# A hybrid mLSTM and pooling block: the o and z projections of two heads as one group of 1024 columns, in which three of eight tile pairs are multiplied by seven products

## The chip, the core and the metric

The kernel runs on one core of one Trainium2 chip. The metric is the device time of one execution in microseconds (us). PE is the matmul engine (PEld its weight loads), DVE the vector engine, ACT the scalar engine, POOL the third elementwise engine, SP the engine whose queue issues the weight transfers. A matmul multiplies a stationary tile of 128x128 with up to 512 moving columns and adds the product to a bank of PSUM (128 x 512 float32).

## The reference, cut to what matters

256 tokens, width 2048, 8 heads of 256, float32 throughout.

```python
h = rmsnorm(x, norm_pre_w)
q, k, v, o_g, z_a, i_pre, f_pre, u_b, z_b, g_a, g_b = split(h @ w_in)   # 2048 columns each for q,k,v,o,z,g_a,g_b; 1024 for u,z_b
q, k = silu(causal_conv4(q)), silu(causal_conv4(k))
h_t  = mlstm_chunkwise(q * 256**-0.5, k, v, i_pre + bi, log_sigmoid(f_pre + bf))
h_t  = rmsnorm_per_head(h_t) * mlstm_norm_w
y_a  = sigmoid(o_g) * h_t * silu(z_a)
y_b  = (multiscale_pool(u_b) @ pool_w) * pool_scale * silu(z_b)
merged = sigmoid(g_a) * (y_a @ w_proj_mlstm) + sigmoid(g_b) * (y_b @ w_proj_pool)
x = x + rmsnorm(merged @ w_out, norm_post_w)
```

Here the chunkwise recurrence is computed with the 256 tokens as two halves of 128 (causal products of q, k and v with a decay matrix E).

## The kernel before

**Precision.** Every float32 operand is split into a high part `wh` (or `xh`) in the matmul's own float format and the remainder `wl` (`xl`), and a product is three matmuls: high with high, low with high, high with low. `hi_lo` does the splitting: ACT casts to the high part (L63), DVE subtracts (L64). The input x lies split in `xc` for the whole kernel (16 tiles of 128 channels, by 256 tokens).

**Weights.** They come as tiles `raw` of 128 x 2048 (1 MB), three of which rotate (`rawp`); SP's queue issues the transfers. Each tile is split in two chunks of 1024 columns; four `wh` and four `wl` rotate (`split`).

**Three ways to multiply.** `tok_block` makes 512 output columns for two halves of the tokens (`t` = 0, 1): x is stationary, the weights move, 96 matmuls (L127, L128, L130) into two `acc` banks. `chan_block` makes 256 output channels by 256 tokens: the weights are stationary, x moves, 64 wide and 64 half-wide matmuls (L147, L149). `group` makes 1024 columns for both halves of the tokens: eight tiles, each a pair of two 128-row blocks (from the upper and the lower half of the contraction) by two blocks of 512 columns. Five of the eight are multiplied plainly (24 matmuls each); three (`NS`) are multiplied by Winograd's form of Strassen's scheme, seven products instead of eight (21 matmuls): DVE forms differences of the four weight blocks (`t13`, `t24`, L673 to L675), the sums of the x blocks (`s_h`, `s_l`) are prepared once by `s_forms`, and the products go to four banks `ps` and four banks `C` and are combined at the end. The order of the eight is 3, 4, 0, 5, 1, 6, 2, 7: the form pairs 0, 1 and 2 stand between plain ones.

**The stages.** (1) `first`: o of heads 0 and 1, with x as it lands; meanwhile `stats` sums the squares of x on ACT (L249), POOL takes the power (`rstd`), and `stats_bc` spreads `rstd` over the partitions by two matmuls with a diagonal matrix `dg` (L264, L265). (2) Eight `chan_block`s for the pooling branch, beside them the gates' projection (`gates`, 16 matmuls of L291) and the pooling itself. (3) Four mLSTM stages j of two heads each, L573: o as a token block (in stage 0 it is there already), the first q block and its convolution (`conv_block`), z, the second q block, v, two k blocks; the attention-like part of the pair (`mlstm_pair`) is a generator that runs in steps between the chunks of the next stage and is emptied by `drain`. (4) Gates g_a and g_b, two token blocks and three groups; then the two projections, with two groups; then the output projection with the last group.

**What sets the order.** The kernel is written as a plain program; a scheduler then orders each engine's instructions by its own estimate of when their inputs are ready, and each engine takes its queue in that order. `tc.keep_in_program_order(i)` pins an instruction behind everything that was written before it on its engine. `const`, `rawp`, `ph1` and `latew` are pools of on-chip memory; a tile of a pool with `bufs=2` has two places that rotate.

Of the kernel before, what the change touches and what calls it, by code (L numbers as in the profile page):

```python
# [10 lines left out]
F32 = mybir.dt.float32  # L11
# [29 lines left out]
def block_kernel(ctx: ExitStack, tc: tile.TileContext, a: dict, out: bass.AP):  # L41
# [217 lines left out]
    def stats_bc():  # L259

        pb = small()
        for t in range(2):
            dg = sp.tile([P, P], F32, name="dg", bufs=2)
            nc.vector.tensor_scalar(dg, ident, rstd[:, t : t + 1], None, op0=ALU.mult)  # L264
            i = nc.tensor.matmul(pb[:, t * P : (t + 1) * P], ones_f, dg, start=True, stop=True)  # L265
            if t == 0:
                tc.keep_in_program_order(i)
        nc.vector.tensor_copy(rstd_bc, pb[:, :T])
# [217 lines left out]
    def mlstm_pair(j, G, qk):  # L486
# [38 lines left out]
        for hh in range(2):  # L525
# [46 lines left out]

    for j in range(4):  # L573
        po = tok_block(xtiles(4 + j), xh, xl) if j else so0
        so = []
        for t in range(2):
            s = gate.tile([P, 512], F32, name="g", tag=f"g{t}") if j else so0[t]
            nc.scalar.activation(s, po[t], AF.Sigmoid, scale=rstd[:, t : t + 1])
            so.append(s)
        pq = chan_block(qtiles(2 * j))  # L580
        drain()
        q = ph1.tile([P, 4, 2, T], F32R, name="q")
        qh, ql = q[:, :, 0], q[:, :, 1]
        kh, kl = (ph1.tile([P, 4, T], F32R, name=n) for n in ("kh", "kl"))
        conv_block(pq, 4 * j, qh, ql, 0)
        pz = tok_block(xtiles(8 + j), xh, xl)
        for t in range(2):
            s = ph1.tile([P, 512], F32, name="sz", tag="sz", bufs=2)
            nc.scalar.activation(s, pz[t], AF.Sigmoid, scale=rstd[:, t : t + 1])
            nc.vector.scalar_tensor_tensor(s, pz[t], rstd[:, t : t + 1], s, op0=ALU.mult, op1=ALU.mult)  # L590
            nc.vector.tensor_tensor(so[t], so[t], s, op=ALU.mult)
        conv_block(chan_block(qtiles(2 * j + 1)), 4 * j + 2, qh, ql, 2)
        pv = tok_block(xtiles(j), xh, xl)
        for t in range(2):
            hi_lo(
                v_h[:, t, :, 0:HD], v_l[:, t, :, 0:HD], pv[t].rearrange("p (h d) -> p h d", h=2),
                rstd[:, t : t + 1],
            )
        conv_block(chan_block(qtiles(8 + 2 * j)), 16 + 4 * j, kh, kl, 0)
        conv_block(chan_block(qtiles(8 + 2 * j + 1)), 16 + 4 * j + 2, kh, kl, 2)  # L600
        side.append(mlstm_pair(j, so, (q, kh, kl)))


    def st(tile_):
        return lambda k, t: tile_[:, k, t * P : (t + 1) * P]

# [17 lines left out]
    def group(gi, st_h, st_l, forms, get_a, get_b):  # L624
# [22 lines left out]
        for kp in order:  # L647
# [26 lines left out]
            nc.vector.tensor_tensor(t24[:, 0], b4[:, 3], t13[:, 0], op=ALU.subtract)  # L674
            nc.vector.tensor_tensor(t24[:, 1], b4[:, 2], t24[:, 0], op=ALU.subtract)  # L675
            flat = [t_.rearrange("p b n -> p (b n)") for t_ in (t13, t24)]
# [40 lines left out]
    for j in range(2):  # L717
        pg = tok_block(xtiles(12 + j), xh, xl)
        for t in range(2):
            gs[0, j, t] = gate.tile([P, 512], F32, name="g", tag=f"g{t}")  # L720
            nc.scalar.activation(gs[0, j, t], pg[t], AF.Sigmoid, scale=rstd[:, t : t + 1])  # L721
    drain()
    ph1_ctx.close()
    latew = ctx.enter_context(tc.tile_pool(name="latew", bufs=1, side="right"))
    lateg_ctx = ExitStack()
    lateg = lateg_ctx.enter_context(tc.tile_pool(name="lateg", bufs=1, side="right"))
    forms = s_forms(lambda part, h: xc[:, 8 * h : 8 * h + NS, part])
    for gi, (n, j0) in enumerate(((1, 0), (0, 2), (1, 2))):
# [10 lines left out]
    for jp in range(2):  # L739
# [184 lines left out]
```

## Time and profile before

| | |
|---|---|
| median of 3 runs | 970.8 us (970.52 to 970.91) |
| the profiled execution | 971.45 us, its span 969.6 us |
| mean granted clock of PE | 0.996 |
| weights read | 184.85 MB, 193 GB/s over the span |

The profiled execution is 0.65 us slower than the median. A line of a timeline has the start in us, the length in us, the engine, the line of the kernel, the operation, the tiles written and read with their shape, how many instructions were merged, and in brackets the idle time before it with what ended that. A row of a group has busy us and the mean ns of one; neighbours on one engine overlap a little, so the pitch from start to start is what counts in a sum.

### The profile page before, as it was taken

What the parts mean: (1) busy time and instruction counts of PE and PEld (TensorE: products, weight loads), DVE (VectorE), ACT (ScalarE), POOL (GpSimd) and SP (SyncE); (2) the same over time, 40 slices, a digit from 0 to 9 for tenths busy, and PEclk for the clock granted to TensorE, in tenths of its full rate; (3) what the DMA queues carried; (4) which work ended last, traced back from release to release, by engine and by line L of the source; (5) the groups of instructions that cost most, each with busy time, mean ns of one, the idle gap of its engine ahead of it and who ended that gap; (6) DMA issues with size and microseconds to landing.
All of it is one profiled execution on the core that took longest, in us unless ns stands there. A gap on an engine that the chain in (4) does not pass through costs nothing.

```text
span 969.6 us, 12590 instructions
## 1 busy us (share of the span) xinstructions
PE 956.9 (99%) x4731; PEld 807.4 (83%) x4731; DVE 746.3 (77%) x1097; ACT 535.5 (55%) x730; POOL 14.5 (1%) x35
## 2 busy tenths in 40 slices
PE   9899999999999999999999999999999999999996
PEld 6788888888888888888888888788888888888886
DVE  7599767667766777668677587779889779789994
ACT  7747544456644466445654476465566455454661
POOL 1000000000000000000000000000000000000001
PEclk9999999999999999999999999999999999999998
DMA  9755545554555544555364633645654654656742
GB/s 349 304 186 172 178 170 200 189 175 174 174 191 199 177 171 162 193 209 174 131 217 173 214 134 131 252 182 183 230 195 145 251 211 144 210 217 248 267 174 88
DMA packets 29309, 187.76 MB, mean 194 GB/s; under 512 B 3264, under 2 KB 3648, under 8 KB 8256
## 3 DMA queue, kind: packets, MB, share of 16 engines
q1 hardware_dynamic: 28816, 183.81, 53.0%
q10 hardware_dynamic: 432, 3.15, 0.9%
q8 instruction: 37, 0.61, 0.2%
q14 instruction: 24, 0.20, 0.1%
HBM read 184.85 MB, written 2.10 MB: 193 GB/s over the span
## 4 chain that ended last, share of the span: by engine, by line
PE 61%; issue 37%; ACT 1%; POOL 0%; DVE 0%; DVEq 0%; ACTq 0%; POOLq 0%
PE acc L147 18%; PE acc L127 10%; PE acc L128 10%; PE acc L130 10%; PE acc L149 9%; PE sm L72 1%; PE sm L73 1%; PE sm L74 1%; PE sm L170 0%; PE sm L291 0%; ACT xw L249 0%; PE sm L564 0%; DVE xr L799 0%; PE sm L513 0%; POOL xr L797 0%
## 5 line engine op out<-in xcount | busy, mean ns | idle before, releaser
L64 DVE TENSOR_TENSOR wl<-raw,wh 128x1024 fp32r<-128x1024 f32 (+1 forms) x328 | 387.0, 1191 | 140.6 <-ACT wh L63 138.5
L63 ACT CAST wh<-raw 128x1024 fp32r<-128x1024 f32 (+1 forms) x328 | 334.7, 1028 | 281.8 <-PE acc L147 96.0
L147 PE MATMUL acc<-xc,wh 128*128 128x512 f32 x768 | 194.3, 395 | 3.0 <-ACT wh L63 3.0
L127 PE MATMUL acc<-wh,xc 128*128 128x512 f32 x448 | 175.8, 392 | 0.0
L128 PE MATMUL acc<-wh,xc 128*128 128x512 f32 x448 | 174.7, 390 | 0.0
L147 PEld LDWEIGHTS acc<-xc,wh 128*128 128x128 f32 x768 | 139.9, 190 | 28.9 <-ACT wh L63 3.2
L130 PE MATMUL acc<-wl,xc 128*128 128x512 f32 x448 | 121.2, 389 | 0.0
L149 PEld LDWEIGHTS acc<-xc,wl 128*128 128x128 f32 x768 | 104.9, 191 | 7.6
L149 PE MATMUL acc<-xc,wl 128*128 128x256 f32 x768 | 107.1, 282 | 0.0
L130 PEld LDWEIGHTS acc<-wl,xc 128*128 128x128 f32 x448 | 84.1, 188 | 17.7
L127 PEld LDWEIGHTS acc<-wh,xc 128*128 128x128 f32 x448 | 84.2, 188 | 17.5 <-ACT wh L63 1.2
L128 PEld LDWEIGHTS acc<-wh,xc 128*128 128x128 f32 x448 | 84.2, 188 | 16.5
L63 ACT CAST wh<-t 128x1024 fp32r<-128x1024 f32 x36 | 37.9, 1052 | 53.5 <-PE acc L643 41.4
L64 DVE TENSOR_TENSOR wl<-t,wh 128x1024 fp32r<-128x1024 f32 x36 | 44.0, 1223 | 20.1 <-ACT wh L63 20.1
L641 PE MATMUL acc<-wh,xc 128*128 128x512 f32 x141 | 55.0, 390 | 0.6 <-ACT g L721 0.6
L643 PE MATMUL acc<-wh,xc 128*128 128x512 f32 x141 | 55.0, 390 | 0.0
L645 PE MATMUL acc<-wl,xc 128*128 128x512 f32 x141 | 40.5, 390 | 0.0
L478 DVE SCALAR_TENSOR_TENSOR cy<-pad,vec,cy 128x256 f32<-128x256 f32 x96 | 39.3, 476 | 0.0
L643 PE MATMUL acc<-wh,y_l 128*128 128x512 f32 x92 | 35.9, 390 | 0.0
L641 PE MATMUL acc<-wh,y_h 128*128 128x512 f32 x92 | 35.8, 390 | 0.0
L641 PEld LDWEIGHTS acc<-wh,xc 128*128 128x128 f32 x141 | 26.5, 188 | 6.6 <-ACT g L721 1.0
L645 PEld LDWEIGHTS acc<-wl,xc 128*128 128x128 f32 x141 | 26.5, 188 | 5.6
(258 smaller groups left out, 1204.9 us busy)
## 6 DMA issues: line engine op xcount, KB each, us to landing
raw<-in_wx SPq DMA_DIRECT2D x52, 1024.0 KB, 4.8
raw<-in_ws SPq DMA_DIRECT2D x48, 1024.0 KB, 4.8
raw<-in_wq SPq DMA_DIRECT2D x44, 1024.0 KB, 4.8
raw<-in_wpp SPq DMA_DIRECT2D x8, 1024.0 KB, 4.7
raw<-in_wo SPq DMA_DIRECT2D x8, 1024.0 KB, 5.3
xw<-in_xw SPq DMA_DIRECT2D x15, 384.0 KB, 6.0
raw<-in_wq SPq DMA_DIRECT2D x8, 512.0 KB, 7.9
xw<-in_x SPq DMA_DIRECT2D x4, 512.0 KB, 8.1
```

Of the source, the lines that this page charges most:

```text
L63: nc.scalar.copy(hi, src)
L64: nc.vector.tensor_tensor(lo, src, hi.bitcast(F32), op=ALU.subtract)
L72: nc.tensor.matmul(ps, lh, rh, start=start, stop=False)
L127: nc.tensor.matmul(ps[t], st_h(k, t), wh[:, cols], start=k == 0, stop=False)
L128: nc.tensor.matmul(ps[t], st_l(k, t), wh[:, cols], start=False, stop=False)
L130: nc.tensor.matmul(ps[t], st_h(k, t), wl[:, cols], start=False, stop=k == n - 1)
L147: nc.tensor.matmul(ps[c], wh[:, cols], xc[:, k], start=k == 0, stop=False)
L149: nc.tensor.matmul(ps[c][:, 1], wl[:, cols], xc[:, k, 0], start=False, stop=k == KT - 1)
L478: nc.vector.scalar_tensor_tensor(y, pad[:, 1 + j : 1 + j + T], cw[:, j : j + 1], y, op0=ALU.mult, op1=ALU.add)
L641: nc.tensor.matmul(dst, lh, wh, start=key not in begun, stop=False)
L643: nc.tensor.matmul(dst, ll, wh, start=False, stop=False)
L645: nc.tensor.matmul(dst, lh, wl, start=False, stop=stop)
```

## The change

Four things change.

1. In the mLSTM stages, o and z of two heads (512 columns each) become one `group` of 1024 columns; in stage 0, where o is there already, v and z do. The stages then run v (from stage 1 on), the first q block, the second q block, the group, two k blocks. `values` splits v as before; `gate_pair` adds the two sums of the group (`C` and `E`) and makes sigmoid(o) * silu(z). The weights' arrays are laid out to match (seven groups of the old order are now numbered from 4). `s_forms` of x is called in stage 0 instead of after the mLSTM stages, and serves the later groups too.
2. Within a form pair the four blocks are differenced otherwise: `t1` (512 columns) is one difference, another is written over block 1 of `raw`, `t24` holds two more. Four subtractions of 512 columns (L639 to L642 in the new file) stand for one of 1024 and two of 512; the chunks are now blocks 2 and 3, blocks 0 and 1, `t1`, `t24`. `t1`, `t24` and `junk` have one place each.
3. `latew`, the pool of these tiles, is opened before the mLSTM stages.
4. `stats_bc` loses `keep_in_program_order`.

```diff
-            i = nc.tensor.matmul(pb[:, t * P : (t + 1) * P], ones_f, dg, start=True, stop=True)
-            if t == 0:
-                tc.keep_in_program_order(i)
+            nc.tensor.matmul(pb[:, t * P : (t + 1) * P], ones_f, dg, start=True, stop=True)
...
+    latew = ctx.enter_context(tc.tile_pool(name="latew", bufs=1, side="right"))
...
-                junk = ph1.tile([P, HD], F32, name="junk", bufs=2)
+                junk = ph1.tile([P, HD], F32, name="junk")
...
-            t13 = latew.tile([P, 2, 512], F32, name="t13", bufs=2)
-            t24 = latew.tile([P, 2, 512], F32, name="t24", bufs=2)
-            nc.vector.tensor_tensor(t13, b4[:, 1:4:2], b4[:, 0:2], op=ALU.subtract)
-            nc.vector.tensor_tensor(t24[:, 0], b4[:, 3], t13[:, 0], op=ALU.subtract)
+            t1 = latew.tile([P, 512], F32, name="t1")
+            t24 = latew.tile([P, 2, 512], F32, name="t24")
+            nc.vector.tensor_tensor(t1, b4[:, 1], b4[:, 0], op=ALU.subtract)
+            nc.vector.tensor_tensor(b4[:, 1], b4[:, 3], b4[:, 1], op=ALU.subtract)
+            nc.vector.tensor_tensor(t24[:, 0], b4[:, 3], t1, op=ALU.subtract)
             nc.vector.tensor_tensor(t24[:, 1], b4[:, 2], t24[:, 0], op=ALU.subtract)
...
-                (raw[:, 0:512], 512, ((0, ps[0], x_(0, 0), last),)),
                 (raw[:, 1024:2048], 1024, (((0, 0), C[0, 0], x_(1, 0), False), ((0, 1), C[0, 1], form(3), False))),
-                (flat[0], 1024, ((1, ps[1], form(0), last), (3, ps[3], form(2), last))),
-                (flat[1], 1024, ((2, ps[2], form(1), last), ((1, 0), C[1, 0], x_(1, 1), False))),
+                (raw[:, 0:1024], 1024, ((0, ps[0], x_(0, 0), last), (3, ps[3], form(2), last))),
+                (t1, 512, ((1, ps[1], form(0), last),)),
+                (t24.rearrange("p b n -> p (b n)"), 1024, ((2, ps[2], form(1), last), ((1, 0), C[1, 0], x_(1, 1), False))),
...
+    def gate_pair(C, E, so):
+        for t in range(2):
+            o, z, r = E[t, 0], E[t, 1], rstd[:, t : t + 1]
+            nc.vector.tensor_tensor(o, C[t, 0], o, op=ALU.add)
+            nc.vector.tensor_tensor(z, C[t, 1], z, op=ALU.add)
+            nc.scalar.activation(so[t], o, AF.Sigmoid, scale=r)
+            nc.scalar.activation(o, z, AF.Sigmoid, scale=r)
+            nc.vector.scalar_tensor_tensor(z, z, r, o, op0=ALU.mult, op1=ALU.mult)
+            nc.vector.tensor_tensor(so[t], so[t], z, op=ALU.mult)
...
+    for j in range(4):
...
+        pv = tok_block(xtiles(j - 1), xh, xl) if j else None
+        pq = chan_block(qtiles(2 * j))
+        drain()
+        if j:
+            for t in range(2):
+                values(t, pv[t])
+        else:
+            forms = s_forms(lambda part, h: xc[:, 8 * h : 8 * h + NS, part])
+        conv_block(pq, 4 * j, qh, ql, 0)
+        conv_block(chan_block(qtiles(2 * j + 1)), 4 * j + 2, qh, ql, 2)
+        C, E = group(j, xh, xl, forms, small, bank)
...
+        conv_block(chan_block(qtiles(8 + 2 * j)), 16 + 4 * j, kh, kl, 0)
+        conv_block(chan_block(qtiles(8 + 2 * j + 1)), 16 + 4 * j + 2, kh, kl, 2)
+        side.append(mlstm_pair(j, so, (q, kh, kl)))
```

How the scheduler's order moves, at two places. First PE's queue from the end of stage 1 on: L130 is the last of o, L147 and L149 a chunk of the first pooling block, L265 the spread of `rstd`, L291 (in the new file L289) the gates. Before, with five more chunks of L147 and L149 in the first gap and four in the second:

```order
L130 MATMUL acc<-wl,xc 128x512 x2
L147 MATMUL acc<-xc,wh 128x512 x8
L149 MATMUL acc<-xc,wl 128x256 x8
...
L265 MATMUL sm<-dg,ones_f 128x128 x2
...
L291 MATMUL sm<-xc,gc_405 128x512 x4
L291 MATMUL sm<-xc,gc_407 128x512 x4
```

and now, with one more chunk in the gap:

```order
L130 MATMUL acc<-wl,xc 128x512 x2
L147 MATMUL acc<-xc,wh 128x512 x8
L149 MATMUL acc<-xc,wl 128x256 x8
...
L265 MATMUL sm<-dg,ones_f 128x128 x2
L289 MATMUL sm<-xc,gc_405 128x512 x4
L289 MATMUL sm<-xc,gc_407 128x512
L147 MATMUL acc<-xc,wh 128x512 x8
```

The spread and five gate matmuls stand behind the second chunk of the first pooling block, where the spread stood behind the sixth; the eleven other gate matmuls follow eight chunks later.

Second DVE's queue after a second q block of a stage: `cy` and `q` are its convolution's results, `wl` the chunks of what PE multiplies next. Before, where v follows:

```order
L478 SCALAR_TENSOR_TENSOR cy<-pad_1384,vec,cy 128x256
L64 TENSOR_TENSOR wl<-raw,wh 128x1024
L483 TENSOR_TENSOR cy<-cy,cs 128x256 x2
L64 TENSOR_TENSOR wl<-raw,wh 128x1024
L64 TENSOR_TENSOR q<-cy,q 128x256 x2
L64 TENSOR_TENSOR wl<-raw,wh 128x1024 x6
L67 SCALAR_TENSOR_TENSOR v_l<-acc,rstd,v_h 128x2x256 x2
```

and now, where the group follows (the first row's `wl` is the fourth plain chunk, the last three rows are the four chunks of form pair 0):

```order
L64 TENSOR_TENSOR wl<-raw,wh 128x1024
L482 TENSOR_TENSOR cy<-cy,cs 128x256 x2
L641 TENSOR_TENSOR t_2769<-raw,t_2768 128x512
L64 TENSOR_TENSOR q<-cy,q 128x256 x2
L642 TENSOR_TENSOR t_2769<-raw,t_2769 128x512
L64 TENSOR_TENSOR wl<-raw,wh 128x1024 x2
L64 TENSOR_TENSOR wl<-t_2768,wh 128x512
L64 TENSOR_TENSOR wl<-t_2769,wh 128x1024
```

The subtractions of the form pair stand between the convolution's steps, and four chunks of a form pair follow where chunks of a plain block did.

More of the change, by code (lines that the diff above doesn't have):

```diff
@@ L571, in mlstm_pair @@
                 )
[L573 to L605, printed above, removed]
     def s_forms(hl):
@@ L669, in group @@
             last = kp == NS - 1
-            t13 = latew.tile([P, 2, 512], F32, name="t13", bufs=2)
-            t24 = latew.tile([P, 2, 512], F32, name="t24", bufs=2)
-            nc.vector.tensor_tensor(t13, b4[:, 1:4:2], b4[:, 0:2], op=ALU.subtract)
-            nc.vector.tensor_tensor(t24[:, 0], b4[:, 3], t13[:, 0], op=ALU.subtract)
+            t1 = latew.tile([P, 512], F32, name="t1")
[3 more added lines that the diff above has]
+            nc.vector.tensor_tensor(t24[:, 0], b4[:, 3], t1, op=ALU.subtract)
             nc.vector.tensor_tensor(t24[:, 1], b4[:, 2], t24[:, 0], op=ALU.subtract)
-            flat = [t_.rearrange("p b n -> p (b n)") for t_ in (t13, t24)]
             form = lambda i: (s_h[:, i, kp], s_l[:, i, kp])
@@ new lines, in values @@
+    def values(t, v):
+        hi_lo(
+            v_h[:, t, :, 0:HD], v_l[:, t, :, 0:HD], v.rearrange("p (h d) -> p h d", h=2), rstd[:, t : t + 1]
+        )
+    for j in range(4):
+        q = ph1.tile([P, 4, 2, T], F32R, name="q")
+        qh, ql = q[:, :, 0], q[:, :, 1]
+        kh, kl = (ph1.tile([P, 4, T], F32R, name=n) for n in ("kh", "kl"))
+        pv = tok_block(xtiles(j - 1), xh, xl) if j else None
[9 more added lines that the diff above has]
+        C, E = group(j, xh, xl, forms, small, bank)
+        if j:
+            so = [gate.tile([P, 512], F32, name="g", tag=f"g{t}") for t in range(2)]
+            gate_pair(C, E, so)
+        else:
+            so = so0
+            for t in range(2):
+                v, z, r = E[t, 0], E[t, 1], rstd[:, t : t + 1]
+                nc.vector.tensor_tensor(v, C[t, 0], v, op=ALU.add)
+                nc.vector.tensor_tensor(z, C[t, 1], z, op=ALU.add)
+                values(t, v)
+                nc.scalar.activation(so[t], so[t], AF.Sigmoid, scale=r)
+                nc.scalar.activation(v, z, AF.Sigmoid, scale=r)
+                nc.vector.scalar_tensor_tensor(z, z, r, v, op0=ALU.mult, op1=ALU.mult)
+                nc.vector.tensor_tensor(so[t], so[t], z, op=ALU.mult)
+        conv_block(chan_block(qtiles(8 + 2 * j)), 16 + 4 * j, kh, kl, 0)
+        conv_block(chan_block(qtiles(8 + 2 * j + 1)), 16 + 4 * j + 2, kh, kl, 2)
+        side.append(mlstm_pair(j, so, (q, kh, kl)))
@@ L704, in merge, with st @@
+    def st(tile_):
+        return lambda k, t: tile_[:, k, t * P : (t + 1) * P]
     def merge(j, t, m):
@@ L717, in block_kernel @@
     for j in range(2):
-        pg = tok_block(xtiles(12 + j), xh, xl)
+        pg = tok_block(xtiles(3 + j), xh, xl)
         for t in range(2):
@@ L723, in block_kernel @@
     ph1_ctx.close()
-    latew = ctx.enter_context(tc.tile_pool(name="latew", bufs=1, side="right"))
     lateg_ctx = ExitStack()
     lateg = lateg_ctx.enter_context(tc.tile_pool(name="lateg", bufs=1, side="right"))
-    forms = s_forms(lambda part, h: xc[:, 8 * h : 8 * h + NS, part])
-    for gi, (n, j0) in enumerate(((1, 0), (0, 2), (1, 2))):
+    for gi, (n, j0) in enumerate(((1, 0), (0, 2), (1, 2)), 4):
         C, E = group(gi, xh, xl, forms, *((bank, small) if gi % 2 == 0 else (small, bank)))
@@ L746, in block_kernel @@
         drain()
-        C, E = group(3 + jp, st(y_h), st(y_l), forms, bank, small)
+        C, E = group(7 + jp, st(y_h), st(y_l), forms, bank, small)
         for (t, c), ps in C.items():
@@ L808, in block_kernel @@
         weigh(t, 1024, 1536, po2[t])
-    C, E = group(5, st(m_h), st(m_l), forms, bank, small)
+    C, E = group(9, st(m_h), st(m_l), forms, bank, small)
     for (t, c), ps in C.items():
@@ L896 @@
         ),
-        "wx": np.concatenate([_tiles(w_in[:, c0:c1], 512, 4) for c0, c1 in ((4096, 10240), (12304, 13328))]),
+        "wx": np.concatenate([_tiles(w_in[:, c0:c1], 512, 4) for c0, c1 in ((4608, 6144), (12304, 13328))]),
         "ws": np.stack(
-            [_pairs(w_in, c0) for c0 in (14352, 13328, 15376)]
+            [
+                _pairs(np.concatenate([w_in[:, c : c + 512] for c in (o, 8192 + 512 * j)], axis=1), 0)
+                for j, o in enumerate((4096, 6656, 7168, 7680))
+            ]
+            + [_pairs(w_in, c0) for c0 in (14352, 13328, 15376)]
             + [_pairs(g["w_proj_mlstm"][0], c0) for c0 in (0, 1024)]
```

## The prediction

> **What bounds the kernel now.** I read the page first, then the stretches of PE's idle time in the order of time, then the busy times by stage, then the vector engine's own order around the q blocks. Names: a tile of 2048 weight columns arrives as `raw`; ACT casts 1024 columns of it to `wh`, DVE makes `wl`, and PE multiplies. I call that a chunk; four `wh`/`wl` pairs rotate, so the splitting can lead PE by four chunks at most.
>
> ```profile
> span 969.6 us, 12590 instructions
> PE 956.9 (99%) x4731; PEld 807.4 (83%) x4731; DVE 746.3 (77%) x1097; ACT 535.5 (55%) x730; POOL 14.5 (1%) x35
> PE   9899999999999999999999999999999999999996
> DVE  7599767667766777668677587779889779789994
> ```
>
> PE has no gap but at the start and the end: the time is the number of matmuls times their pitch, plus the start. So a matmul fewer is time won, as long as DVE, second at 77%, keeps up. Three of the four mLSTM stages look alike to a tenth of a microsecond; the first row below is one of them, from the first matmul of o to the first of the next o. The other is a stretch in which the old groups run one after the other.
>
> ```profile
> 220.12:336.40 116.28, 116.28 (x599) 99.27 (x598) 82.42 (x140) 63.76 (x95) 1.39 (x2) 1.00 0.51 181
> 683.00:704.00 21.00, 21.00 (x93) 17.26 (x92) 18.02 (x19) 12.96 (x14) 0.00 (x0) 1.00 0.55 202
> ```
>
> The columns are length, then busy PE, PEld, DVE, ACT, POOL, the granted clock, DMA share and GB/s. The stage leaves DVE 33.9 us idle. The groups run DVE at 18.0 of 21.0 us (86%), and PE still loses nothing: this is the nearest measure of what the new stage asks for.
>
> **Three pairs by seven products.** A plain pair of tiles costs 24 matmuls, a form pair 21. Starts of a plain pair, of a form pair, and of what follows, in one old group:
>
> ```profile
> 635.31 0.39 PE L641 MATMUL acc<-wh,xc 128*128 128x512 f32 x1
> ...
> 640.76 0.39 PE L641 MATMUL sm<-wh,xc 128*128 128x512 f32 x1
> ...
> 645.61 0.39 PE L641 MATMUL acc<-wh,xc 128*128 128x512 f32 x1
> ```
>
> 5.45 us against 4.85 us: 0.60 us a pair. Four new groups with three form pairs each take 12 x 0.60 = 7.2 us off PE. (9 matmuls at the plain pitch of 5.45/24 = 0.227 us would be 2.04 us a group; the form pair runs a little slower a matmul, 0.231 us, so I take the measured 1.8.) The bytes don't change: a stage loads 20 tiles of 1 MB before and after.
>
> **What DVE pays for it.** Per form pair: four subtractions of 512 columns, and 3584 columns to split where a plain pair has 2048. Per group: eight additions of 512 columns (four that combine the products, four that add the two sums). The prices by pitch, start to start:
>
> ```profile
> 622.33 0.69 DVE L674 TENSOR_TENSOR t<-raw,t 128x512 f32<-128x512 f32 x1
> 622.94 0.69 DVE L64 TENSOR_TENSOR wl<-raw,wh 128x512 fp32r<-128x512 f32 x1
> ```
>
> A 512-column operation takes 0.61 us of the queue, a 1024-column split 1.14 (below, 265.20 to 266.34). So 12 x 0.61 = 7.3 for the subtractions, 3 x (1.14 + 0.61) = 5.3 for the extra splits, 8 x 0.61 = 4.9 for the additions: 17.5 us a stage. v and z keep their own work (`values`, and the gate's multiply). DVE goes from 82.4 to 99.9 us in a stage that PE finishes in 116.3 - 1.8 = 114.5: 87%, the share of the old groups. ACT gains three casts of 1024 and three of 512 columns and two copies of 512, eight operations of 1.03 us at most (row 34.99 below): 8 us on 63.8, far off. On the average all of it lies beside PE.
>
> The tight place is the group's entry. Two q blocks now come in a row before it, and the second one's convolution must pass through DVE ahead of the first form pair's splits; before, plain chunks of z or v followed. This is the old pattern after a q block that PE ended at 259.32:
>
> ```profile
> 259.32 0.40 PE L127 MATMUL acc<-wh,xc 128*128 128x512 f32 x1
> 260.85 0.74 DVE L413 TENSOR_TENSOR pad<-pad,acc 128x256 f32<-128x256 f32 x2
> 262.83 2.45 DVE L478 SCALAR_TENSOR_TENSOR cy<-pad,vec,cy 128x256 f32<-128x256 f32 x6
> 265.20 1.21 DVE L64 TENSOR_TENSOR wl<-raw,wh 128x1024 fp32r<-128x1024 f32 x1
> 266.34 0.75 DVE L483 TENSOR_TENSOR cy<-cy,cs 128x256 f32<-128x256 f32 x2
> 268.14 0.77 DVE L64 TENSOR_TENSOR q<-cy,q 128x256 fp32r<-128x256 f32 x2
> 268.82 1.22 DVE L64 TENSOR_TENSOR wl<-raw,wh 128x1024 fp32r<-128x1024 f32 x1
> ```
>
> Counted from PE's end of the second q block: the convolution starts at 1.53 and gives DVE back at 5.88 (265.20); the fourth plain chunk's split ends at 7.0; then, in the new order, the cy pair (266.34 to 268.14 less a split: 0.66), one subtraction (0.61), the q pair (268.14 to 268.82: 0.68), one subtraction (0.61), and the first form chunk's split (1.14): 10.7 to 10.8. PE has two plain pairs (10.9 us) and four matmuls (0.9) to do before it asks for that `wl`, at 11.8. About 1.0 us is left, and the next three splits keep 1.3, 1.6 and 1.6 us by the same count. So I cost the entry at nothing; the bounds are 0 and, were DVE 2.5 us later than counted, 1.5 us in each of the four stages, 6 us.
>
> At the group's end four bank sums, two multiplies and two products (5 us) fall beside the first k block, whose splits (4 x 1.14) have 11.2 us of PE (rows 131.92 and 143.08 below) to hide in. v's two banks wait through the first q block for `values` (two operations of 512 columns on either engine); the next block wants the banks 11 us later. The single buffers of `t1`, `t24` and `junk` only order work that one engine does in that order anyway, and the four small subtractions of the old groups take as long as the one large and two small ones they replace.
>
> **The forms of x, moved up to the last pooling blocks.** Their DVE work, by the rows below, is 2 x 0.95 + 4 x 0.55 + 1.76 = 5.9 us, and they hold two of the three `raw` tiles for a while.
>
> ```profile
> 110.00:140.00 30.00, 30.00 (x181) 26.75 (x180) 23.39 (x43) 14.22 (x21) 0.18 (x3) 1.00 0.47 172
> ...
> 121.08 1.23 DVE L64 TENSOR_TENSOR wl<-raw,wh 128x1024 fp32r<-128x1024 f32 x1 [0.22 <-ACT wh L63]
> 131.92 1.99 PE L147 MATMUL acc<-xc,wh 128*128 128x512 f32 x8
> 143.08 0.40 PE L127 MATMUL acc<-wh,xc 128*128 128x512 f32 x1
> ...
> L612 DVE TENSOR_TENSOR raw<-xc 128x768 f32<-128x768 f32 x4 | 3.7, 951 | 0.0
> L616 DVE TENSOR_TENSOR raw<-raw 128x384 f32<-128x384 f32 x3 | 1.7, 553 | 0.0
> L64 DVE TENSOR_TENSOR s_l<-raw,s_h 128x1536 fp32r<-128x1536 f32 x3 | 5.3, 1755 | 2.0 <-ACT s_h L63 2.0
> ...
> raw<-in_wq SPq DMA_DIRECT2D x44, 1024.0 KB, 4.8
> ```
>
> DVE is idle for 6.6 of those 30 us, so 5.9 fits. It also leads: the split at 121.08 is that of the first q block's first chunk, which PE takes at 131.92, 10.8 us later. A tile lands 4.8 us after its issue, and PE eats one in 5.6 (a q block of two tiles runs from 131.92 to 143.08), so a tile fewer for some 5 us costs part of that lead. I take nothing; the upper bound is one landing, 4.8 us.
>
> **The edge on the spread of 1/rms.** Without it the two L265 and five of the sixteen gate matmuls (L291, in the new file L289) go ahead of the block's third chunk, into the gap in which PE now waits for ACT:
>
> ```profile
> 30.65 0.66 DVE L64 TENSOR_TENSOR gc<-gw,gc 128x64 fp32r<-128x64 f32 x4 [3.96 <-ACT gc L63]
> 31.96 1.11 PE L149 MATMUL acc<-xc,wl 128*128 128x256 f32 x8
> 33.62 0.71 POOL L197 TENSOR_TENSOR rstd<-rs_tmp,mhalf 128x2 f32<-128x2 f32 x1 [29.55 <-DVE rs_tmp L196]
> 34.36 0.48 DVE L264 TENSOR_SCALAR dg<-ident,rstd 128x128 f32<-128x128 f32 x2 [0.82 <-POOL rstd L197]
> 34.99 1.03 ACT L63 CAST wh<-raw 128x1024 fp32r<-128x1024 f32 x1
> 36.07 3.69 PE L147 MATMUL acc<-xc,wh 128*128 128x512 f32 x8 [3.00 <-ACT wh L63]
> 40.55 2.00 PE L147 MATMUL acc<-xc,wh 128*128 128x512 f32 x8
> 48.93 0.60 PE L265 MATMUL sm<-dg,ones_f 128*128 128x128 f32 x4
> 49.29 2.11 PE L147 MATMUL acc<-xc,wh 128*128 128x512 f32 x8
> 60.57 3.89 PE L291 MATMUL sm<-xc,gc 128*128 128x512 f32 x16
> 64.29 1.98 PE L147 MATMUL acc<-xc,wh 128*128 128x512 f32 x8
> ...
> 620.35 0.50 PE L641 MATMUL acc<-wh,xc 128*128 128x512 f32 x1 [0.57 <-ACT g L721]
> ```
>
> L265 takes 0.36 us (48.93 to 49.29), five gate matmuls 5/16 of 3.72 = 1.16: 1.52 us leave their old places. `dg` is there at 34.84, the gate weights since 31.3, so they end at 34.84 + 1.52 = 36.36, where the third chunk began at 36.07: 1.23 us won. The chunk's eight matmuls took 3.69 us after the gap and 2.00 a little later, because the granted clock had dropped:
>
> ```profile
> 36.07:37.00 0.93, 0.93 (x2) 0.81 (x3) 0.93 (x1) 0.93 (x2) 0.00 (x0) 0.53 0.03 13
> 40.00:42.00 2.00, 2.00 (x13) 1.74 (x13) 2.00 (x2) 0.85 (x1) 0.00 (x0) 1.00 0.76 287
> ```
>
> With work from about 34.7 on, PE idles 1.6 us where it idled 3.0. Whether the clock still drops no row says: 0 and 1.69 us are the bounds. I take 1.69, since nowhere else in this trace does a gap under 3 us come before a low clock (the gap of 0.57 us at 620.35 is the only other one, and the clock stays full).
>
> [...]
>
> **Sum**, against the profiled execution of 971.45 us (span 969.6): 971.45 - 7.2 - 1.23 - 1.69 = 961.3. The median of the runs, 970.8, lies 0.65 below that execution, so the forecast is 960.7.
>
> **Rivals.**
> 1. The clock drops all the same: 1.69 comes back, 962.4. [...] Against it: PE works again for more than a microsecond before the point at which the clock was lost.
> 2. DVE comes a little late at the group's entry, by up to 2.5 us, and PE waits up to 1.5 us in each stage: 962 to 967. For it: 1.0 us is a thin margin, built from pitches of a pattern that never ran in this order. Against it: four chunks of lead, and the old groups at the same share.
> 3. The other side: DVE's queue waits in order, so that an ACT result that comes late (the sigmoid of the convolution behind two casts, the q casts) holds every split behind it. From a lateness of 1.0 + 10.1/4 = 3.5 us at each entry the change loses; at 6 us PE waits 5 us in each stage, 20 us in all, and the gaps, longer than 3 us, cost another 1.69 each: 960.7 + 20 + 6.8 = 987. Against it: a stage gives DVE 14.6 us idle, and in the old pattern the q pair starts right behind the split ahead of it, with no wait. [...]
> 4. The forms move costs a landing (4.8 us): 965.5.
> 5. The change yields nothing, because DVE's bound eats just the 7 to 10 us: 970.8.
>
> **How the numbers follow.** Forecast 0.64 (960.7, its own range 959.5 to 961.8), rival 1 0.15, rival 2 0.10, rival 4 0.03, rival 5 0.02, rival 3 0.06. The range 959.0 to 966.5 holds the forecast, rivals 1 and 4 and most of 2, and leaves out about 1 in 10. A difference under 0.2% (1.9 us) is about what a measurement here can't tell from none. Faster by more: 0.64 + 0.15 + 0.10 + 0.03 = 0.92; within 0.2%: 0.02; slower: 0.06.
>
> **What the new profile would show.** Right: form pairs in the stages at 4.85 us; a stage of 114.5 us with PE busy throughout and DVE near 100 us; the gap at 33 us cut to about 1.6, L265 and five gate matmuls in it, and the next eight matmuls in 2.0 us at clock 1.00. Wrong: PE idle before a `wl` or `wh` at the first form chunk (rivals 2, 3), a low clock after 36 us (rival 1), a cast that waits for `raw` near 140 us (rival 4).

## The result: 963.2 us against 970.9, and where the missing 2.5 us of the forecast went

The changed kernel takes 963.22 us (median of four runs, 962.85 to 963.42); the kernel before took 970.86 in the same comparison. The ratio is 0.9924, with a 95% interval of 0.9908 to 0.994. That is 7.6 us faster where 10.1 was forecast: inside the range of 959.0 to 966.5, 2.5 us above the likeliest value and outside the 959.5 to 961.8 that the forecast had for itself. The profiled execution took 963.42 us, 8.03 less than that of before.

First the head of the page of the changed kernel: span, busy times, and the rows of PE and DVE in forty slices.

```profile
span 961.6 us, 12726 instructions
PE 949.4 (99%) x4695; PEld 799.1 (83%) x4695; DVE 813.0 (85%) x1219; ACT 556.8 (58%) x761; POOL 14.5 (2%) x35
PE   9999999999999999999999999999999999999996
DVE  7699889897898869988798986678889779879994
```

DVE went from 77% to 85%, and PE's row shows no hole: the second slice of the kernel before (an 8) is now a 9.

Next, busy times by stretch: one mLSTM stage, and within the stage before it the group alone.

```profile
330.42:444.97 114.55, 114.55 (x589) 97.54 (x588) 98.83 (x166) 69.62 (x103) 1.38 (x2) 1.00 0.52 184
266.23:308.10 41.87, 41.87 (x186) 34.37 (x184) 38.51 (x54) 24.34 (x31) 0.00 (x0) 1.00 0.54 191
```

PE is busy for the whole stage, and DVE works 98.8 us of it (99.9 had been counted). Inside the group DVE is busy 92% of the time, and PE still waits for nothing. PE's starts of a plain pair, a form pair and the next plain pair in the group of stage 0:

```profile
157.15 0.39 PE L607 MATMUL sm<-wh,xc 128*128 128x512 f32 x1
...
162.59 0.39 PE L607 MATMUL sm<-wh,xc 128*128 128x512 f32 x1
...
167.45 0.39 PE L607 MATMUL sm<-wh,xc 128*128 128x512 f32 x1
```

The plain pair takes 5.44 us, the form pair 4.86. PE in the start, ahead of the pooling blocks:

```profile
8.59 0.50 PE L127 MATMUL acc<-wh,xc 128*128 128x512 f32 x1 [0.56 <-ACT wh L63]
...
32.35 1.11 PE L149 MATMUL acc<-xc,wl 128*128 128x256 f32 x8
35.10 0.71 PE L265 MATMUL sm<-dg,ones_f 128*128 128x128 f32 x4 [1.63 <-DVE dg L264]
35.56 1.41 PE L289 MATMUL sm<-xc,gc 128*128 128x512 f32 x5
36.81 1.98 PE L147 MATMUL acc<-xc,wh 128*128 128x512 f32 x8
```

The gap is 1.63 us, the spread and five gate matmuls follow, and the next eight matmuls take 1.98 us: the granted clock was 1.00 from 36.81 to 38.80 us. The first row is a wait for a cast in the first block of o, which the profiled execution of before did not have; its pooling blocks begin 0.39 us later (27.75 for 27.36).

The loss that I had not foreseen is late in the kernel. These are the three late groups and the first projection block behind them, before and then changed (two views):

```profile
618.71:766.68 147.97, 147.40 (x647) 121.01 (x646) 127.83 (x138) 86.68 (x97) 0.00 (x0) 1.00 0.56 205
```

```profile
609.41:758.49 149.08, 148.16 (x646) 120.81 (x645) 125.74 (x143) 85.48 (x96) 0.00 (x0) 1.00 0.55 198
```

The stretch grew by 1.11 us, though the kernel before lost 0.57 us in it at 620.35 (the sigmoid's wait of the prediction), which is gone. What is new stands at its end. First the kernel before, in the timelines of DVE, of SP's queue (the issue of a transfer), of ACT and of PE:

```profile
737.64 0.55 DVE L618 TENSOR_TENSOR raw<-raw 128x384 f32<-128x384 f32 x1
738.11 1.22 DVE L64 TENSOR_TENSOR wl<-raw,wh 128x1024 fp32r<-128x1024 f32 x1
...
738.26 0.33 SPq L105 DMA_DIRECT2D raw<-in_wpp  x1
...
743.05 2.01 ACT L63 CAST wh<-raw 128x1024 fp32r<-128x1024 f32 x2 [2.12 <-DMA raw<-in_wpp]
...
744.92 0.39 PE L127 MATMUL sm<-wh,yb_h 128*128 128x512 f32 x1
```

and the same place in the changed kernel:

```profile
728.68 1.22 DVE L64 TENSOR_TENSOR wl<-raw,wh 128x1024 fp32r<-128x1024 f32 x1
729.82 0.68 DVE L664 TENSOR_TENSOR e<-sm,e 128x512 f32<-128x512 f32 x1
730.41 0.55 DVE L584 TENSOR_TENSOR raw<-raw 128x384 f32<-128x384 f32 x1
...
729.93 0.33 SPq L105 DMA_DIRECT2D raw<-in_wpp  x1
...
734.75 1.05 ACT L63 CAST wh<-raw 128x1024 fp32r<-128x1024 f32 x1 [2.21 <-DMA raw<-in_wpp]
...
735.85 0.50 PE L127 MATMUL sm<-wh,yb_h 128*128 128x512 f32 x1 [0.50 <-ACT wh L63]
...
738.38 1.20 PE L130 MATMUL sm<-wl,yb_h 128*128 128x512 f32 x4 [0.41 <-DVE wl L64]
```

L618 (in the new file L584) is the fourth sum of `s_forms` of y. Before, it stood ahead of DVE's last split of the group. It gave the first working tile, one of three `raw` buffers, back at 738.19, and SP issued the projection block's first weight tile at 738.26, 6.66 us ahead of PE's first matmul of that block. Now it stands behind that split and an addition of the group (L664). The first weight tile takes the buffer of the group's last tile instead, which that split gives back at its end (729.90). SP issues the tile at 729.93, 5.42 us ahead of the time at which PE would have begun (735.85 less its wait, 735.35). In both kernels the cast starts 4.8 us after the issue, so the 0.8 us that were to spare have become PE's wait for the cast. The second wait is for a low part: DVE has `s_l` and four products in its queue ahead of that split, which it reaches at 737.11.

So the profiled execution, 2.1 us above the forecast of 961.3, adds up: 0.39 us in the first block, 0.44 in the four groups (they won 4 x 1.69 us for 7.2), 1.11 in the late stretch, 0.19 in the last three groups (41.84 for 41.78 twice, 64.12 for 64.05 from the start of the last group to PE's last matmul). The other 0.4 us lie between profile and median: the profiled execution was 0.65 us above the median before and is 0.2 above it now.

### The profile page after: what moved, and what is told of

It reads as the page before. It is cut to its first block, busy times and chain, and to the rows that moved or that the text cites. A ratio compares the mean times of both kernels' runs of the same rounds, so it can differ in the third digit from the quotient of the medians.

```text
span 961.6 us, 12726 instructions
## 1 busy us (share of the span) xinstructions
PE 949.4 (99%) x4695; PEld 799.1 (83%) x4695; DVE 813.0 (85%) x1219; ACT 556.8 (58%) x761; POOL 14.5 (2%) x35
## 3 DMA queue, kind: packets, MB, share of 16 engines
q10 hardware_dynamic: 432, 3.15, 0.9%
## 4 chain that ended last, share of the span: by engine, by line
PE 93%; issue 4%; DVE 1%; POOL 1%; ACT 0%; DVEq 0%; POOLq 0%; ACTq 0%
PE acc L147 18%; PE acc L149 9%; PE sm L609 7%; PE sm L607 7%; PE sm L611 7%; PE acc L607 7%; PE acc L609 7%; PE acc L611 7%; PE acc L127 4%; PE acc L128 4%; PE acc L130 4%; PE sm L130 2%; PE sm L127 2%; PE sm L128 2%; PE sm L72 1%
## 5 line engine op out<-in xcount | busy, mean ns | idle before, releaser
L63 ACT CAST wh<-raw 128x1024 fp32r<-128x1024 f32 x328 | 339.6, 1051 | 217.3 <-PE acc L147 65.6
L64 DVE TENSOR_TENSOR wl<-raw,wh 128x1024 fp32r<-128x1024 f32 x328 | 395.0, 1222 | 57.7 <-ACT wh L63 57.2
L147 PE MATMUL acc<-xc,wh 128*128 128x512 f32 x768 | 192.6, 393 | 0.0
L147 PEld LDWEIGHTS acc<-xc,wh 128*128 128x128 f32 x768 | 138.7, 189 | 25.3
L149 PEld LDWEIGHTS acc<-xc,wl 128*128 128x128 f32 x768 | 104.8, 190 | 7.5
L149 PE MATMUL acc<-xc,wl 128*128 128x256 f32 x768 | 107.1, 282 | 0.0
L609 PE MATMUL sm<-wh,xc 128*128 128x512 f32 x239 | 93.3, 391 | 0.0
L607 PE MATMUL sm<-wh,xc 128*128 128x512 f32 x239 | 93.2, 390 | 0.0
L64 DVE TENSOR_TENSOR wl<-t,wh 128x512 fp32r<-128x512 f32 (+1 forms) x60 | 57.0, 957 | 27.8 <-ACT wh L63 21.8
L127 PE MATMUL acc<-wh,xc 128*128 128x512 f32 x192 | 76.2, 397 | 0.6 <-ACT wh L63 0.6
L128 PE MATMUL acc<-wh,xc 128*128 128x512 f32 x192 | 75.0, 391 | 0.0
L611 PE MATMUL sm<-wl,xc 128*128 128x512 f32 x239 | 68.9, 390 | 0.0
L607 PE MATMUL acc<-wh,xc 128*128 128x512 f32 x153 | 59.8, 391 | 0.0
L609 PE MATMUL acc<-wh,xc 128*128 128x512 f32 x153 | 59.8, 391 | 0.0
L130 PE MATMUL acc<-wl,xc 128*128 128x512 f32 x192 | 52.8, 390 | 0.0
L607 PEld LDWEIGHTS sm<-wh,xc 128*128 128x128 f32 x239 | 44.9, 188 | 9.5
L609 PEld LDWEIGHTS sm<-wh,xc 128*128 128x128 f32 x239 | 44.9, 188 | 9.4
L611 PE MATMUL acc<-wl,xc 128*128 128x512 f32 x153 | 45.3, 390 | 0.0
L127 PEld LDWEIGHTS acc<-wh,xc 128*128 128x128 f32 x192 | 36.1, 188 | 8.4 <-ACT wh L63 1.8
L130 PEld LDWEIGHTS acc<-wl,xc 128*128 128x128 f32 x192 | 36.0, 188 | 7.7
```

The lines of the kernel that those rows point to most:

```text
L63: nc.scalar.copy(hi, src)
L64: nc.vector.tensor_tensor(lo, src, hi.bitcast(F32), op=ALU.subtract)
L127: nc.tensor.matmul(ps[t], st_h(k, t), wh[:, cols], start=k == 0, stop=False)
L128: nc.tensor.matmul(ps[t], st_l(k, t), wh[:, cols], start=False, stop=False)
L130: nc.tensor.matmul(ps[t], st_h(k, t), wl[:, cols], start=False, stop=k == n - 1)
L147: nc.tensor.matmul(ps[c], wh[:, cols], xc[:, k], start=k == 0, stop=False)
```

## The experiments

Each run stands beside runs of the kernel before on the same chip, whose medians were 971.0, 971.5, 971.6 and 971.1 us in the four sets. The changed kernel was run in the first comparison alone, where the kernel before took 970.9, so a difference of up to some 0.7 us between a later run and its 963.2 says nothing by itself.

### The parts alone: edge_only, group_only

```diff
 (kernel before)
-            if t == 0:
-                tc.keep_in_program_order(i)
```

> The kernel before with the edge on the spread of 1/rms taken away and nothing else. My theory: this is worth the start's part of the sum alone, 1.23 us of filled gap and 1.69 us of clock: 970.9 - 2.9 = 968.0 us, with PE's gap at 33 us cut from 3.0 to 1.6 us and the next eight matmuls in 2.0 us at a clock of 1.00. Rival: the clock drops here all the same, and only the filled gap is won: 969.6, with those eight matmuls at 3.7 us. Rival: the start gives what it wins back later (the other eleven gate matmuls and the pooling chain behind them wait): 970.9.

Measured: 967.87 us (six runs, 967.72 to 968.07), ratio 0.997 (0.9959 to 0.9981), 3.15 us less. PE waits 1.63 us at 34.93, and the next eight matmuls take 1.99 us. The opposite edit:

```diff
 (changed kernel)
+            if t == 0:
+                tc.keep_in_program_order(i)
```

> The changed kernel with the edge on the spread of 1/rms put back: the group, the new differences and the moved forms of x without the start's part. My theory: the parts add up, so 963.2 + 2.9 = 966.1 us, the 3.0 us gap with its half clock is back, the four groups still take 41.87 us each, and the two short waits of PE at the first projection block (0.5 and 0.4 us) are there again. Rival: the 0.4 us that the changed kernel lost before its first pooling chunk comes from the new order of the start; then they are gone here and the time is 965.7.

Measured: 966.29 us (965.73 to 967.4), ratio 0.9956 (0.9944 to 0.9968), 4.73 us less. The gap is 3.00 us again with 3.52 us for the next eight matmuls, and both late waits are there (0.70 and 0.23 us). The parts add up: 3.15 + 4.73 = 7.88 us, against 7.6 for both together. The wait in the first block is missing here, but its length follows no edit: the pooling blocks begin between 27.15 and 28.07 us in the profiles of these kernels, whose first block is the same. So the 0.39 us are chance. The rival of 965.7 is not told apart from my 966.1 by the time; the profile of edge_only, with the new order of the start and no wait there, decides against it.

### The group without form pairs: all_plain

```diff
+        ns = 0 if gi < 4 else NS
-        rest = list(range(NS, 8))
+        rest = list(range(ns, 8))
...
```

The additions of the two sums behind the group become copies, since there is only one sum.

> The changed kernel with all eight pairs of the four new groups multiplied plainly (192 matmuls in place of 183, no differences, no product banks); everything else, the new order of the stages too, stays. My theory: the group's gain is the matmuls and nothing else, 4 x 1.69 = 6.8 us (a group of 41.87 us against two token blocks of 21.78 us each): 963.2 + 6.8 = 970.0 us, stages of 116.2 us with DVE back near 82 us. Rival: the order of the stages (v and the q blocks first) gains or loses by itself; then the stage is not 116.2 us.

Measured: 970.01 us (twelve runs), ratio 0.999 (0.9982 to 0.9999). A stage and a group:

```profile
333.98:450.22 116.24, 116.24 (x599) 99.24 (x597) 84.69 (x144) 63.85 (x95) 1.38 (x2) 1.00 0.51 181
384.35:427.90 43.55, 43.55 (x195) 36.06 (x193) 25.53 (x33) 18.60 (x23) 0.00 (x0) 1.00 0.57 203
```

The stage takes what it took before the change, so the new order of the blocks gains and costs nothing by itself. The form pairs are worth 43.55 - 41.87 = 1.68 us a group, 0.56 us each.

### The new differences alone: diffs_only

The diff's second part, put into the kernel before.

> The kernel before with the new differences alone (four subtractions of 512 columns, chunks of blocks 2 and 3, blocks 0 and 1, t1, t24) in its six groups. My theory: the two late waits of PE in the changed kernel (0.5 and 0.4 us of marked idle time at the first projection block, some 1.2 us of pitch in all) come from here: DVE reaches the forms of y later by the queue, their buffer is given back late, and a weight tile lands late. So 970.9 + 0.6 to 0.9 = 971.6 us, with a wait for a cast at the first projection block. Rival: the subtractions cost nothing (970.9), and the waits come from the other order in front of the late groups.

Measured: 973.97 us (five runs, 973.22 to 974.28), ratio 1.0032 (1.0021 to 1.0044): 2.95 us more, three to five times what I had named. The late stretch with the projection block (the sum of two windows), and PE in the start and late:

```profile
sum 149.12, PE 148.20 PEld 120.77 DVE 128.25 ACT 85.37 POOL 0.00; mean PE 74.10 PEld 60.38 DVE 64.13 ACT 42.69 POOL 0.00
```

```profile
36.35 3.78 PE L147 MATMUL acc<-xc,wh 128*128 128x512 f32 x8 [3.00 <-ACT wh L63]
39.93 1.91 PE L149 MATMUL acc<-xc,wl 128*128 128x256 f32 x8
41.64 2.45 PE L147 MATMUL acc<-xc,wh 128*128 128x512 f32 x8
...
746.77 0.50 PE L127 MATMUL sm<-wh,yb_h 128*128 128x512 f32 x1 [0.61 <-ACT wh L63]
749.19 1.20 PE L130 MATMUL sm<-wl,yb_h 128*128 128x512 f32 x4 [0.31 <-DVE wl L64]
```

149.12 us, as in the changed kernel, with the same two waits, and DVE has the same order there: the fourth sum stands behind the group's last split, and the first weight tile is issued when that split ends. The late loss comes from the new differences and from nothing in the stages. It is 1.15 us here and 0.19 us in the last groups; of the rest in this profile, 1.24 us is a longer low clock after the 3.00 us gap (6.82 us at a granted clock of 0.50, with 19 matmuls begun in them, where the profile of before has 3.41 us and eight) and 0.28 us the first block. Why all five runs lie so high stays open: the mean granted clock of the other four, 0.996 to 0.997, is that of the kernel before, so a longer low clock does not explain them.

### Places of their own for the sums: own_place

```diff
-    def s_forms(hl):
+    def s_forms(hl, pool=None):
-        f = rawp.tile([P, 2048], F32, name="raw")[:, : 2 * NS * T]
+        f = (pool.tile([P, 2 * NS * T], F32, name="f") if pool else rawp.tile([P, 2048], F32, name="raw")[:, : 2 * NS * T])
```

with the same for `r`, the second working tile, and `lateg` as the pool in the two calls for y and m.

> The changed kernel with the sums of y and of m (s_forms' two working tiles) in places of their own instead of two of the three rotating weight buffers; the additions, the products and PE's order stay. My theory: the waits at the first projection block come from a weight tile that can be fetched only when the fourth sum (L584), late in DVE's queue, gives its buffer back; with places of their own the tile is there early, both waits go, and the late groups with the first projection block take 147.5 instead of 149.1 us: 963.2 - 1.5 = 961.7 us. Rival: DVE itself is late there (86% busy, with 5 us of sums and splits in front of that block); then PE waits for a split instead of a cast and the time stays at 962.7 to 963.2.

Measured: 962.01 us (961.65 to 962.03), ratio 0.9902 (0.9888 to 0.9915), 1.2 us under the changed kernel. The late stretch (the sum of two windows), then DVE, SP's queue and ACT ahead of the projection block:

```profile
sum 147.54, PE 147.54 PEld 121.00 DVE 122.24 ACT 85.35 POOL 0.00; mean PE 73.77 PEld 60.50 DVE 61.12 ACT 42.68 POOL 0.00
```

```profile
728.61 1.23 DVE L64 TENSOR_TENSOR wl<-raw,wh 128x1024 fp32r<-128x1024 f32 x1 [0.17 <-ACT wh L63]
...
719.89 0.33 SPq L105 DMA_DIRECT2D raw<-in_wpp  x1
...
729.44 1.06 ACT L63 CAST wh<-raw 128x1024 fp32r<-128x1024 f32 x1
```

The first weight tile is issued at 719.89, 10 us earlier, and cast from 729.44 on, 5.9 us ahead of PE's need at 735.34; both waits are gone. The edit did more than I had written, though. Without the rotating buffers the sums run far earlier in DVE's queue, at 591.7 to 600.4 us, and DVE is busy 3.5 us less in the stretch (122.24 for 125.74). For the first wait the buffers are the cause all the same: the group's last split starts at 728.61, where it started at 728.68, so DVE was no earlier there (it had idle time and waited 0.17 us for the cast), and the tile no longer waited for it. For the second wait this run can't tell the early weights from DVE's lighter queue. My theory had the right place but the wrong releaser: the fourth sum holds up the second weight tile (issued at 730.99 in the changed kernel), and the wait came from the first.

### How near the entry is: entry_3, entry_8

```diff
-            nc.vector.tensor_scalar(y, pad..., op0=ALU.mult, op1=ALU.add)
+            for _ in range(1 + extra):   # second q block: 3 or 8
+                nc.vector.tensor_scalar(y, pad..., op0=ALU.mult, op1=ALU.add)
```

> The changed kernel with three more repeats of the convolution's first step (L473, two instructions of 256 columns, 0.65 us a pair by pitch) in the second q block of each stage: 2.0 us more of DVE just ahead of the group's entry, the result unchanged. My theory: the first form chunk's split is ready 1.8 us before PE asks for it (276.2 against 278.0 in the changed kernel's stage 1), so PE waits 0.1 to 0.2 us in each stage at most: 963.2 to 964.0 us. Rival: the margin is the 1.0 us that I had counted, and PE waits 1.0 us in each stage: 967.2.

Measured: 963.4 us (962.99 to 963.76), no wait of PE in any stage. In the changed kernel the rows of the entry are these (DVE, then PE):

```profile
266.90 0.75 DVE L411 TENSOR_TENSOR pad<-pad,acc 128x256 f32<-128x256 f32 x2
...
274.99 2.36 DVE L64 TENSOR_TENSOR wl<-raw,wh 128x1024 fp32r<-128x1024 f32 x2
```

```profile
278.06 0.39 PE L611 MATMUL sm<-wl,xc 128*128 128x512 f32 x1
```

The first of the two splits ends at 274.99 + 1.22 = 276.2, PE asks for it at 278.06: a margin of 1.8 us. In entry_3 that split ends at 278.48 and PE asks for it at 278.68, because one more high product now stands ahead of it in PE's order; 0.2 us of the margin is left.

> The same with eight repeats, 5.2 us more of DVE in each stage. In PE's order the low products of the fourth plain chunk and of the first form chunks now stand behind the high products of the next chunks, so PE has 11 matmuls (2.5 us) more to do before it asks for them. My theory: PE waits about 5.2 - 1.8 - 1.7 = 1.7 us in each stage, and the lateness is then caught up, since a stage leaves DVE 10 us idle even so: 963.2 + 4 x 1.7 = 970.0 us. Rival (the third of the prediction): DVE's queue in its order holds every split behind the late ones; then PE waits 3.4 us or more in each stage, and gaps of that length cost clock too: 976.6 to 983.

Measured: 971.72 us (ten runs), 8.5 us more, so the change's whole gain is lost. Stage 1, ACT and PE:

```profile
282.56 1.05 ACT L63 CAST wh<-t 128x1024 fp32r<-128x1024 f32 x1 [1.54 <-DVE t L643]
```

```profile
283.66 0.50 PE L608 MATMUL acc<-wh,s_h 128*128 128x512 f32 x1 [1.57 <-ACT wh L63]
```

PE waits 1.57 us in each stage and loses 2.1 in each (from one such wait to the next 116.65 us, where a stage took 114.55). The size is near mine, the place is not: PE waits for a high part, since ACT's cast of `t24` needs the subtraction (L643) that stands behind the convolution in DVE's queue. 3.4 us or more were not seen, nor a low clock after a 1.57 us gap (behind the one in stage 1 the matmuls start 0.23 us apart, as ahead of it, and the mean granted clock of the execution is 0.998).

### The clock and the length of the gap: gap, gap_long

```diff
+        r2 = sp.tile([P, 2], F32, name="r2")
+        nc.gpsimd.tensor_copy(r2, rstd)          # gap_long: five copies in a row
...
-            nc.vector.tensor_scalar(dg, ident, rstd[:, t : t + 1], None, op0=ALU.mult)
+            nc.vector.tensor_scalar(dg, ident, r2[:, t : t + 1], None, op0=ALU.mult)
```

> The changed kernel with one copy of 1/rms by POOL put ahead of the spread, so that PE's first gap grows from 1.6 us to some 2.3 us (POOL's power took 0.71 us). [...]

Measured: 964.08 us (963.94 to 964.87), where 963.2 + 0.7 = 963.9 had been forecast. The copy took 0.18 us, not 0.7, and added 0.25, so this was a weak test: the gap was 1.88 us.

```profile
35.39 0.71 PE L267 MATMUL sm<-dg,ones_f 128*128 128x128 f32 x4 [1.88 <-DVE dg L266]
...
36.86 2.01 PE L147 MATMUL acc<-xc,wh 128*128 128x512 f32 x8
```

In this execution the eight matmuls behind the gap took 2.01 us, and no clock was lost there; the runs are 0.5 to 1.4 us above what the longer gap explains, and whether some of them lost clock I can't tell.

> The changed kernel with five copies of 1/rms by POOL ahead of the spread, in a row: PE's first gap, 1.63 us there and 1.88 us with one copy, becomes some 2.3 to 2.9 us. [...] Rival: there is a sharp length between 1.9 and 3.0 us; then either all runs or none lose the 1.2 to 3 us of clock.

Measured: 966.23 us (965.46 to 967.35).

```profile
36.44 0.71 PE L271 MATMUL sm<-dg,ones_f 128*128 128x128 f32 x4 [2.87 <-DVE dg L270]
...
37.46 3.48 PE L147 MATMUL acc<-xc,wh 128*128 128x512 f32 x8
```

The gap grew by 1.24 us and the median by 3.0. The profiled execution shows where most of the other 1.8 us went: the granted clock was half from 37.61 to 41.02 us (0.80 over the microsecond from 37 on, 0.50 over each of the next three, 0.99 from 41 to 42), which is 1.7 us of work. The forecast of 963.9 to 964.5, which is 963.2 and the 0.7 to 1.3 us by which the gap was to grow, failed. The mean granted clock of the five runs goes from 0.994 in the slowest to 0.998 in the fastest, so some lose more than others. That speaks against the rival's "all runs or none"; whether fewer lose it than after 3.00 us five runs can't say.

### More gain: gates_first, four_pairs, four_pairs_gap

All three have the places of their own for the sums of y and m.

```diff
 gates_first: in stats()
+        while not gated:
+            yield 1
         stats_bc()
 in gates(): no steps ahead of the products, then
+        gated.append(1)
+        while not ready:
+            yield 1
```

with the edge on the spread put back.

> The kernel with places of their own for the sums of y and m, and the sixteen gate matmuls ahead of the spread: they need the gates' weights (split by 31.7 us in the changed kernel) and x, not 1/rms, and now stand in PE's first gap (33.5 to 35.1 us); the spread follows three chunks later. My theory: the gap goes, and its 1.63 us with it: 962.0 - 1.6 = 960.4 us. Rival: the pooling chain, which needs the spread, comes later by 8 us and its banks hold up PE in the third or fourth pooling block; then 962.0 or more, with a new wait before 60 us.

Measured: 964.83 us (963.72 to 966.98), 2.8 us above own_place. The rival happened, at another place (PE, then DVE):

```profile
32.86 3.89 PE L292 MATMUL sm<-xc,gc 128*128 128x512 f32 x16
...
62.06 1.93 PE L149 MATMUL acc<-xc,wl 128*128 128x256 f32 x8 [2.93 <-DVE wl L64]
```

```profile
55.94 1.73 DVE L317 RECIPROCAL row<-row 8x256 f32<-8x256 f32 x1
...
60.82 1.19 DVE L64 TENSOR_TENSOR wl<-raw,wh 128x1024 fp32r<-128x1024 f32 x1
```

The gap at 33 us is closed, but between 55.94 and 60.82 us ten steps of the gates and of a pooling block, now side by side, stand in DVE's queue ahead of one split, PE waits 2.93 us for it, and the matmuls behind are slow again (the eight at 62.06 take 1.93 us, where the eight at 66.97 take 1.11).

```diff
 four_pairs
+        ns = 4 if gi in (0, 1, 2, 3) else NS
```

and the sums of x for four pairs; `e12`, `e21` lie in `t24`.

> The same with four form pairs instead of three in the four groups of the stages (order 4, 5, 0, 6, 1, 7, 2, 3; the sums of x for four pairs; two of the four result tiles lie in t24). My theory: a form pair is worth 0.56 us as long as DVE has room, and a stage of 114 us has it (98.8 + 4.2 = 103 us, 90%): 960.4 - 4 x 0.56 = 958.2 us. Rival: pairs 2 and 3 follow each other and ask DVE for 6.5 us each in 4.9 us of PE; with the lead gone PE waits up to 3 us in each stage, and the time is 962 to 970.

Measured: 962.55 us (962.5 to 964.32), 2.28 us under gates_first, with the same wait at 62 us (2.95): four times 0.57 as expected, though the runs of gates_first alone spread over 3.3 us, and on a base that was not what I had thought. Last, the four pairs without the gates' move:

> The kernel with places of their own for the sums of y and m and with four form pairs in the stages' groups, the gates left where the changed kernel has them (five matmuls in the first gap, eleven later). My theory: the parts that worked add up and the late wait of the kernels with the gates first (2.9 us at 62 us) is gone: 962.0 - 4 x 0.57 = 959.7 us, PE's gap at 33 us again 1.6 us, groups of 41.29 us. Rival: that wait was due to the four pairs' sums of x or to the buffers' order rather than to the gates; then it stays, and the time is 962 us or more.

Measured: 959.45 us (958.95 to 959.6), ratio 0.9878 (0.9861 to 0.9895). It beats both kernels, the changed one by 3.8 us, and the wait at 62 us is gone, so it belonged to the gates' move. A stage and a group:

```profile
329.29:443.27 113.98, 113.98 (x587) 96.96 (x585) 103.13 (x174) 71.40 (x105) 1.38 (x2) 1.00 0.52 185
379.66:420.95 41.29, 41.29 (x182) 33.80 (x181) 39.87 (x55) 24.68 (x32) 0.00 (x0) 1.00 0.53 189
```

DVE is busy 39.87 of the group's 41.29 us (97%), and PE still waits for nothing.

## Why the prediction was right, and which step failed

- **The number.** 963.2 us lies in the range, but in its upper part, which stood there for rivals 1, 2 and 4, and none of them came as named. About half of the missing 2.5 us went to a wait that the prediction had put at nothing. That the range held is in part luck; the mechanism of the gain, matmuls saved while DVE keeps up and a gap filled, is not.
- **Form pairs, 7.2 us.** The mechanism is shown by all_plain and, at the size of 0.57 us, by four_pairs; the term was 0.4 to 0.5 us too large. I had subtracted one form pair from one plain pair of an old group (5.45 - 4.85 = 0.60). A group against eight plain pairs gives 0.56.
- **The spread and the gate matmuls, 1.23 + 1.69 us.** Right: 3.15 us alone in edge_only; the pooling blocks and the q blocks up to the first group took 2.94 us less than before by the profiles. Rival 1 is refuted for this gap (1.98 and 1.99 us for the next eight matmuls). My ground for taking 1.69 in full, one gap of 0.57 us with a full clock, was thin, since gap_long loses clock after 2.87 us (0.50 for 3.41 us); that 1.63 us was short enough could not be known from the trace of before. The second number is a mean, though: with the edge the kernel before ran from 969.0 to 972.7 us in 18 runs, without it from 967.7 to 968.1 in six.
- **DVE, 99.9 us a stage, and the entry.** Right and a little careful: 98.8 us, and a margin of 1.8 us for 1.0. The convolution began 0.67 us behind PE's end of the q block (266.23 to 266.90), where I had carried over 1.53 from the old pattern. Rivals 2 and 3 did not happen; entry_8 shows that the mechanism exists, and that 5.2 us at each entry would have eaten the gain.
- **The forms of x.** Costed at nothing, and there is no wait of PE near 140 us: right.
- **The step that failed** is the sentence that the four small subtractions "take as long as the one large and two small ones they replace". The length was about right (DVE was busy 0.4 us more in the late stretch of diffs_only); what I left out is where the others behind them come to stand in DVE's queue. The fourth sum of y, which had stood ahead of the group's last split, came behind it; the projection block's first weight tile went to a buffer that comes free only when that split ends, and was issued 5.42 us ahead of PE's need where it had been 6.66; and PE waited. diffs_only shows this with no change in the stages. It is akin to rival 4 (the forms hold transfer buffers), at the forms of y instead of those of x. It costs 1.3 us net by the profile, and own_place wins 1.2 back.
- **The first block's 0.39 us** differs from run to run and belongs to no step.

## What to carry to other kernels

When an edit replaces instructions by others of the same total length, follow what stands behind them in the queue up to the one that gives a transfer buffer back; a transfer hangs on that one (here it was issued at 729.93 us, when the split ended at 729.90), not on the sum of the lengths. Read from the transfer queue which instruction released each transfer: the one that looks late need not be the one that was waited for. A helper that borrows a rotating transfer buffer for its sums should have a place of its own at the seams of a kernel whose matmul engine never waits. An average of 86% or even 97% on the second engine says little; the margin at the tightest entry, counted row by row and tried by adding work of known length, says how much more can be put there.

## What the runs showed of the hardware that I had not expected

- After a gap of PE of 2.87 us (gap_long) the granted clock fell to 0.50, and eight matmuls took 3.48 us; after 3.00 us they took 3.5 to 3.8, after 1.88 us 2.01, after 1.63 us 1.98 to 2.00.
- What one and the same 3.00 us gap costs differs by execution: the granted clock was 0.50 for 3.41 us in the profile of before and for 6.82 us in that of diffs_only. The two stretches, with the columns of the other window rows (the third number from the right is the granted clock):

```profile
36.12:39.53 3.41, 3.41 (x8) 2.76 (x9) 3.08 (x3) 3.35 (x4) 0.00 (x0) 0.50 0.01 2
```

```profile
35.74:42.56 6.82, 6.21 (x19) 5.24 (x20) 5.35 (x5) 5.06 (x6) 0.00 (x0) 0.50 0.36 121
```

  In gap_long it was low for 3.41 us too (37.61 to 41.02). The wait of 2.93 us in gates_first and that of 2.95 in four_pairs were followed by eight low products in 1.93 and 2.07 us, and by ten high ones in 3.34 and 4.31 us, where eight take 2.00 a little later. What decides how long the clock stays low after a gap, and whether it falls at all, the runs don't show. The kernels with the 3.00 us gap spread over 1.1 to 3.7 us, edge_only over 0.35.
- A POOL copy of 128x2 in a chain added 0.25 us to the gap (0.18 us listed), where POOL's power of the same shape takes 0.71.
